# A table that shifts the ranks of 77 groups of instructions before one more ordering pass

## The chip, the cores and the metric

The program runs on one core of a Trainium2 chip. The metric is the time of one execution on the device, in microseconds, as the median of several executions.

A core has five instruction queues that matter here. TensorE (PE) multiplies matrices and transposes, VectorE (DVE), ScalarE (ACT) and GpSimd (POOL) do elementwise work, and SyncE (SP) issues the transfers between memory and the core's buffers. Each works through its own list of instructions in the order in which they were issued, and waits at an instruction until what it reads is there and what it overwrites is no longer needed.

## What is computed

One layer of a streaming encoder, for a prompt of 2048 tokens and a sample of 32 tokens, with a model width of 1024 in float32. The reference, cut down:

```python
def layer(x, mem):
    h = rmsnorm(x, g_pre_mix)
    qa, ka, va, qb, kb, vb, log_a, r = mix_inputs(h, w_in, w_alpha2, b_alpha)
    oa = chunk_band_prompt(qa, ka, va, rel_bias)      # 8 heads x 64, chunks of 64, band of 9 chunks
    ob, state = gla_recurrence(qb, kb, vb, log_a, s0) # 4 heads, keys of 64, values of 128
    x = x + rmsnorm(mix_output(oa, ob, r, g_gla_out, w_o), g_post_mix)
    mk, mv = mem_kv(mem, g_mem, w_mk, w_mv)           # 256 memory tokens
    x = x + rmsnorm(mem_attention(rmsnorm(x, g_pre_mem), mk, mv, w_mq, w_mo), g_post_mem)
    x = x + rmsnorm(swiglu(rmsnorm(x, g_pre_ffn), w_gate, w_up, w_down), g_post_ffn)  # hidden 2816
```

The outputs are both token streams, the new keys and values of both attentions, and the recurrent states.

## The kernel before

**Arithmetic.** A float32 product is done as three matmuls on operands that are split into a rounded part and a remainder (`mm3`, line 531; its matmuls are the rows of L536). `split` (line 494) makes the two parts: ACT casts the rounded part (L495), and DVE or POOL subtracts it from the raw tile for the remainder (L496). `split_own` (L500, L501) does the same in place for the operands of the output projection. The large products use seven sub-products in place of eight, as in Strassen's scheme: sums of operand quarters (L590 and L593, the helpers `sub` and `add`) stand ahead of the splits, and the results land in PSUM tiles called X, Y, Z, T, W.

**Stages, in order of time.** First the combined input projection, to about 525 us. Then the band attention and the gated linear attention together with the output projection, to about 1210; the folding of the memory's keys and values runs between them. Then the memory attention with its norms, to about 1660, and the FFN to the end.

**Names that the prediction speaks of.**
- `g7_j` and `ha2_j`: operands of the memory attention's scores, memory side and token side (`scores_pair`, from line 1753). `hm2_0` and `hm2_1` are the raw tiles that `ha2_j` is split from. `msX`, `msY`, `msZ` are score tiles, `mst` and `mpr` the softmax's minimum and its result (L1784, L1789), `mpt` the transposes of the result on PE (L1793).
- `wo3_6_4_s`: weights of the output projection for token block 3 and output tile 6, second half; `wops3_6_0` is the product (L1464), `om` its token operand, `sqa` and `acc1` the square sums of the norm behind it, and `y1` its result, scaled in L1517.
- `u14_6`: scores plus bias with the running minimum (L1176) for the band attention; `s` are the scores (L1192), `ks` the loaded keys.
- `n3_7` and `n4_7`: the two norms behind the memory attention for the last 256 tokens (`output`, from line 1880). `n4_s7` sums squares on DVE (L593), PE adds over the partitions with a matmul by ones (L1899), ACT takes the root, and `my7_j`, the tokens, are scaled on DVE (L1910), first with `g_post_mem`, later with `g_pre_ffn`. Between the two POOL adds the residual.
- `wg0_2_s0`: split weights of the FFN's gate, block 0, group 2; `pg0_2_X` are its products. `wu` and `pu` are the same for the up projection.
- `mkps`: products for the memory's keys.

**What sets the order.** The program is first written out in the order of its loops. `Order.queue` (line 426) then sorts it anew. It reads all instructions as a graph (`_read`), and plays them through in a planner with an estimated cost for each (`_pass`, line 296): whenever an engine is free, the ready instruction with the lowest priority number starts there. Ten turns of a pass forward and a pass backward over the graph alternate; a backward pass gives the priorities of the next forward pass, as distances from the end, in planned nanoseconds. The forward pass with the earliest planned end is kept. Its planned starts give the order in each engine's list, which is then fixed by a dependency from each instruction to the one before it on its engine. So nothing is reordered while the program runs: an instruction that waits holds up all that is behind it on that engine.

Of the kernel before, what the change touches and what calls it, by code (L numbers as in the profile page):

```python
# [47 lines left out]
class Order:  # L48
# [12 lines left out]
    LOAD = 1280.0  # L61
    TABLES = {1: "natural_log_exp_and_others", 2: "silu_and_others"}
    ROOM = (208 * 1024, 16 * 1024)

    def __init__(self, tc):
        self.tc = tc
        self.block = tc.nc.cur_bb
        self.hints = {}
        self.edge = mybir.DependencyInfo(mybir.DependencyClass.NoSync, mybir.DependencyReason.DATA)
# [124 lines left out]
    def _read(self, traced):  # L194
# [17 lines left out]
        for ins in traced:  # L212
            kind = type(ins).__name__
            eng = str(ins.engine).split(".")[-1]
            if ins.name in opened:
                p, space, size, right = opened[ins.name]
                lo = max([q[2] for q in stack.values() if q[0] == space and not q[3]], default=0)
                if right:
                    lo = min([q[1] for q in stack.values() if q[0] == space and q[3]], default=self.ROOM[space == PSUM]) - size
                stack[p] = (space, lo, lo + size, right)  # L220
# [200 lines left out]
    def behind(self, late, early):  # L421

        for x in late:
            self.hints.setdefault(x.ins.name, []).extend(y.ins.name for y in early)

    def queue(self):
        self._read(self.block.bb.instructions)
        n = len(self.ops)
        best = None
        prio = self.prio  # L430
        for turn in range(self.PASSES + 1):
            start, end = self._pass(prio)
            if best is None or max(end) < best[0]:
                best = (max(end), start)
            if turn == self.PASSES:
                break
            back, fin = self._pass([-(s + d) for s, d in zip(start, self.dur)], back=end)
            whole = max(fin)
            prio = [whole - b for b in fin]
        start = best[1]  # L440
        order = sorted(range(n), key=lambda i: (start[i], i))
        act = [i for i in order if self.eng[i] == 1]
        tail, table, since, loads = {}, 1, 0, {}
        for p, i in enumerate(act):
            if self.table.get(i, table) != table:
                table = self.table[i]
                gaps = [start[act[q]] - start[act[q - 1]] - self.dur[act[q - 1]] for q in range(since, p + 1)]
                room = [g >= self.LOAD for g in gaps]
                loads[act[since + (room.index(True) if True in room else gaps.index(max(gaps)))]] = table
            if i in self.table:  # L450
                since = p + 1
        for i in order:
            e = self.eng[i]
            if e == self.GATE:
                continue
            todo = list(self.ops[i])
            if i in loads:
                todo.insert(0, self.tc.nc.scalar.preload_act_table_set(self.TABLES[loads[i]]).ins)
            for ins in todo:
                if e in tail:  # L460
                    self.tc.add_manual_dep(ins, tail[e].name, self.edge, reason="order of issue")
                tail[e] = ins
# [2124 lines left out]
```

## Time and profile before

| what | value |
|---|---|
| median of 3 runs | 2976.96 us (2975.37 to 2981.22) |
| the profiled execution | 2977.21 us |
| its span, first to last instruction | 2975.4 us |
| mean granted clock of TensorE | 0.994 |
| idle time of PE in the span | 52.8 us |
| transfers | 586.23 MB, 197 GB/s over the span |

Times within the kernel are microseconds from the start of the span. A row of the timeline has the start, the time, the engine, the line, the operation with its output and inputs by name (buffer numbers left out), how many instructions it stands for, and in brackets how long the engine was idle before it and what ended that. A row of the waits has the total, the number of waits and the longest.

### The profile page before, as it was taken

The page shows a single profiled execution, that of the slowest core. Times are in us where ns is not written, and L with a number is a line of the kernel's source. Part 1 is how long each engine was busy: PE and PEld are TensorE (multiplying, and loading weights), DVE is VectorE, ACT ScalarE, POOL GpSimd, SP SyncE. Part 2 cuts the span into 40 slices and gives each one's busy share as a digit, 9 for nine tenths or more (in the row PEclk, how much of TensorE's full clock was granted, in tenths as well). Part 3 has the DMA queues.
Part 4 walks back from the last instruction along what each step waited for, and adds up shares of the span by engine and source line. Part 5 has one row for each costly group of instructions (what it writes and reads, how often), then busy time and mean ns, then how long its engine had stood idle before and what let it go on. Part 6 is the DMA issues. An engine that isn't in the chain of part 4 may idle for free. (4 is left out here: it accounts for less than half of the span.)

```text
span 2975.4 us, 56400 instructions
## 1 busy us (share of the span) xinstructions
PE 2922.6 (98%) x21011; PEld 2753.1 (93%) x21011; DVE 2253.8 (76%) x4156; ACT 1578.4 (53%) x3374; POOL 853.8 (29%) x991
## 2 busy tenths in 40 slices
PE   9999999999999998999999999999999999999999
PEld 7899999888879787878999999999999999999999
DVE  6488876576777867885678977889977778987775
ACT  5565655576767766665445444445443335443334
POOL 0210000456766655222133211114221113321113
PEclk9999999999999999999999999999999999999999
DMA  9645674986778768545994643454554445543344
GB/s 319 203 166 181 219 232 152 301 279 184 251 234 254 238 192 284 185 167 179 344 313 140 192 159 125 170 177 155 179 174 136 146 156 168 160 173 132 132 154 176
DMA packets 429644, 586.23 MB, mean 197 GB/s; under 512 B 49013, under 2 KB 318606, under 8 KB 429338
## 3 DMA queue, kind: packets, MB, share of 16 engines
q1 hardware_dynamic: 428966, 581.93, 59.6%
q8 instruction: 165, 2.70, 0.4%
q14 instruction: 109, 0.89, 0.1%
q10 hardware_dynamic: 404, 0.71, 0.1%
HBM read 426.46 MB, written 160.33 MB: 197 GB/s over the span
## 5 line engine op out<-in xcount | busy, mean ns | idle before, releaser
L496 POOL TENSOR_TENSOR u<-g,u 128x692 fp32r<-128x692 f32 (+1 forms) x109 | 197.0, 1813 | 896.5 <-ACT u L495 849.4
L536 PE MATMUL pg_X<-mf,wg_s 128*128 128x346 f32 (+1 forms) x1584 | 276.8, 322 | 1.4 <-DVE g L593 0.9
L536 PE MATMUL pu_X<-mf,wu_s 128*128 128x346 f32 (+1 forms) x1584 | 274.2, 320 | 0.0
L536 PEld LDWEIGHTS pg_X<-mf,wg_s 128*128 128x128 f32 x1584 | 256.4, 189 | 2.6 <-DVE g L593 1.1
L536 PEld LDWEIGHTS pu_X<-mf,wu_s 128*128 128x128 f32 x1584 | 255.0, 188 | 0.1
L536 PE MATMUL pdX<-u,wd 128*128 128x346 f32 (+1 forms) x1440 | 234.0, 322 | 0.0
L536 PEld LDWEIGHTS pdX<-u,wd 128*128 128x128 f32 x1440 | 230.5, 189 | 0.2
L1464 PE MATMUL wops<-om,wo_s 128*128 128x512 f32 (+1 forms) x960 | 214.6, 363 | 12.5 <-DVE wo_s L496 4.1
L495 ACT CAST wg_s<-wg_r 128x512 fp32r<-128x512 f32 x231 | 136.7, 620 | 168.7 <-DVE wg_r L590 76.6
L495 ACT CAST u<-g 128x692 fp32r<-128x692 f32 (+1 forms) x109 | 82.8, 773 | 229.2 <-PE pdX L536 190.5
L536 PE MATMUL mo<-pT,hT 128*128 128x256 f32 x1536 | 192.3, 285 | 0.7 <-POOL pT L501 0.7
L536 PEld LDWEIGHTS mo<-pT,hT 128*128 128x128 f32 x1536 | 186.7, 192 | 6.4 <-issue 3.3
L495 ACT CAST wu_s<-wu_r 128x512 fp32r<-128x512 f32 x231 | 136.4, 621 | 99.6 <-DVE wu_r L590 43.5
L496 DVE TENSOR_TENSOR wu_s<-wu_r,wu_s 128x512 fp32r<-128x512 f32 x231 | 171.6, 768 | 21.5 <-ACT wu_s L495 21.4
L1464 PEld LDWEIGHTS wops<-om,wo_s 128*128 128x128 f32 x960 | 153.4, 190 | 36.4 <-POOL om L501 5.1
L496 DVE TENSOR_TENSOR wg_s<-wg_r,wg_s 128x512 fp32r<-128x512 f32 x231 | 157.8, 706 | 34.9 <-ACT wg_s L495 34.2
L593 DVE TENSOR_TENSOR acc<-acc,pdX 128x346 f32<-128x346 f32 (+1 forms) x192 | 97.2, 513 | 60.1 <-PE pdX L536 59.6
L536 PE MATMUL pg_Y<-mf,wg_s 128*128 128x346 f32 (+1 forms) x792 | 138.8, 323 | 0.0
L536 PE MATMUL pu_Y<-mf,wu_s 128*128 128x346 f32 (+1 forms) x792 | 136.9, 321 | 0.0
L536 PEld LDWEIGHTS pg_Y<-mf,wg_s 128*128 128x128 f32 x792 | 128.1, 189 | 0.7 <-ACT g L2184 0.3
L536 PEld LDWEIGHTS pu_Y<-mf,wu_s 128*128 128x128 f32 x792 | 127.6, 188 | 0.0
L1379 POOL TENSOR_TENSOR g_W<-g_W,g_kq 128x128 f32<-128x128 f32 x224 | 110.2, 527 | 59.8 <-ACT g_W L1371 49.5
(578 smaller groups left out, 7203.9 us busy)
## 6 DMA issues: line engine op xcount, KB each, us to landing
wd<-wdd SPq DMA_DIRECT2D x182, 512.0 KB, 5.3
wg_r<-in_w_ffn_gate_dram SPq DMA_DIRECT2D x66, 512.0 KB, 4.2
wu_r<-in_w_ffn_up_dram SPq DMA_DIRECT2D x66, 512.0 KB, 4.6
q<-qd SPq DMA_DIRECT2D x32, 512.0 KB, 6.0
wo_r<-in_w_o_dram SPq DMA_DIRECT2D x64, 256.0 KB, 4.2
wdd<-wds SPq DMA_DIRECT2D x28, 512.0 KB, 5.9
wdd<-wd SPq DMA_DIRECT2D x28, 512.0 KB, 4.1
nb<-nbd SPq DMA_DIRECT2D x16, 640.0 KB, 6.6
```

What stands on the lines that cost most here:

```text
L495: ACT.copy(hi, src)
L496: (lo_eng or DVE).tensor_tensor(out=lo, in0=src, in1=hi.bitcast(F32), op=ALU.subtract)
L536: r = PE.matmul(ps, lhsT=a, rhs=b, start=first and i == 0, stop=last and i == len(seq) - 1, skip_group_check=skip)
L593: eng.tensor_tensor(out=out, in0=a, in1=b, op=ALU.add)
L1379: POOL.tensor_tensor(out=wl, in0=wl, in1=both, op=ALU.mult)
L1464: PE.matmul(ps, lhsT=a, rhs=b, start=i == 0, stop=i == len(seq) - 1)
```

## The change

A table gives numbers to 77 groups of instructions, where a group is what one engine writes into one tile (28 on PE, 11 on ACT, 33 on DVE, 2 on POOL, 3 on SP). `_rank` looks an instruction up by its engine and the tile that it writes. The ten turns run as before; then one more forward pass runs with the priorities of the best pass, each plus its number from the table, negative numbers meaning earlier. Its order is issued unless its planned end is later than that of the best pass. The instructions, the tiles and the planned costs are the same. Lines of the code below the table move by 36.

```diff
+    RANKS = {
+        "PE": {
+            "g11_tt": -4400, "gps011": -2150, "hps200": -1400, "hps300": -31200, "mkps0": -37250, "msX1": -350, "msX7": -70800,
...
+        "DVE": {
...
+            "u14_6_sb": -2750, "u14_7_sb": -34600, "u15_6_sb": -13650, "wg0_1_r0": -32200, "wg0_1_s0": -1550, "wg0_1_s1": -32200,
...
+    }
+    def _rank(self, i):
+
+        for a in self.ops[i][0].outs if self.ops[i][0] is not None else ():
+            if hasattr(a, "bass_ap"):
+                return self.RANKS.get(self.ENGINES[self.eng[i]], {}).get(a.bass_ap.tensor.name.rpartition("_")[0], 0.0)
+        return 0.0
+
     def queue(self):
...
             if best is None or max(end) < best[0]:
-                best = (max(end), start)
+                best = (max(end), start, prio)
...
-        start = best[1]
+        start, end = self._pass([p + self._rank(i) for i, p in enumerate(best[2])])
+        if max(end) > best[0]:
+            start = best[1]
```

The pass moves more than the 77 groups, since each place that changes moves the neighbours too: some 3500 of PE's 18985 instructions, 1300 of DVE's 4158, 900 of ACT's 3108, 230 of POOL's and 500 of SP's stand elsewhere than before, most by one or two places. From the FFN's second group of weights on (about 1720 us) the order is the same. Three places follow.

**The scores of the memory attention (1260–1283 us).** DVE before: ha2_0, the first token operand of score pair 2, stands behind the sums of the norm (y1_3, acc1_3) and the softmax of pair 1.

```order
L1787 RECIPROCAL mst1_11_16926<-mst1_11_16926 128x2
L1789 TENSOR_SCALAR mpr1_11_16927<-mpr1_11_16927,mst1_11_16926 128x256 x2
L1787 RECIPROCAL mst1_00_16947<-mst1_00_16947 128x2
L1789 TENSOR_SCALAR mpr1_00_16948<-mpr1_00_16948,mst1_00_16947 128x256 x2
L593 TENSOR_TENSOR acc1_3_15868<-acc1_3_15868,sqb_3_5_16911 128x544
L1787 RECIPROCAL mst1_10_16998<-mst1_10_16998 128x2
L1789 TENSOR_SCALAR mpr1_10_16999<-mpr1_10_16999,mst1_10_16998 128x256
L496 TENSOR_TENSOR ha2_0_17017<-hm2_0_17013,ha2_0_17017 128x512
L590 TENSOR_TENSOR hm2_0_17013<-hm2_0_17013 128x4x128
L593 TENSOR_TENSOR hm2_0_17013<-hm2_0_17013,hm2_1_17014 128x4x128
```

DVE after, from the end of the first minimum search of pair 1 on (the ISA rows, of L1820):

```order
L1820 ISA mst1_01_16875 128x1
L532 TENSOR_TENSOR ha2_0_17017<-hm2_0_17013,ha2_0_17017 128x512
L626 TENSOR_TENSOR hm2_0_17013<-hm2_0_17013 128x4x128
L629 TENSOR_TENSOR hm2_0_17013<-hm2_0_17013,hm2_1_17014 128x4x128
L1820 ISA mpr1_11_16927,mst1_11_16926<-msX1_16802,msc1_1_16806 128x256
L1820 ISA mst1_11_16926 128x1
L1820 ISA mpr1_11_16927,mst1_11_16926<-msX1_16802,msc1_1_16806 128x256
L1820 ISA mst1_11_16926 128x1
L1823 RECIPROCAL mst1_01_16875<-mst1_01_16875 128x2
L1825 TENSOR_SCALAR mpr1_01_16876<-mpr1_01_16876,mst1_01_16875 128x256
L629 TENSOR_TENSOR y1_3_2_15866<-y1_3_2_15866,x0r3_5_16906 128x544
L629 TENSOR_TENSOR acc1_3_15868<-acc1_3_15868,sqb_3_3_16847 128x544
```

The split of ha2_0 and the two sums on hm2_0 have moved ahead of the second minimum search and of what followed it.

PE before, at the same place (msX1, msZ1: scores of pair 1; msX2: those of pair 2):

```order
L536 MATMUL msZ1_16804<-g7_5_16555,ha1_5_16796 128x512 x12
L1793 MATMUL mpt0_10_16891<-ident_61,mpr0_10_16752 128x128 x4
L536 MATMUL msX1_16802<-g7_6_16568,ha1_6_16799 128x512 x12
L1793 MATMUL mpt1_01_16972<-ident_61,mpr1_01_16876 128x128 x2
L536 MATMUL msX2_17042<-g7_0_15735,ha2_0_17017 128x512 x2
L1793 MATMUL mpt1_01_16972<-ident_61,mpr1_01_16876 128x128 x2
L1793 MATMUL mpt1_11_16979<-ident_61,mpr1_11_16927 128x128 x4
L1793 MATMUL mpt1_00_17112<-ident_61,mpr1_00_16948 128x128 x4
L1793 MATMUL mpt1_10_17119<-ident_61,mpr1_10_16999 128x128 x2
L536 MATMUL msX2_17042<-g7_0_15735,ha2_0_17017 128x512 x8
```

PE after:

```order
L572 MATMUL msZ1_16804<-g7_5_16555,ha1_5_16796 128x512 x11
L1829 MATMUL mpt0_10_16891<-ident_61,mpr0_10_16752 128x128 x4
L572 MATMUL msX2_17042<-g7_0_15735,ha2_0_17017 128x512 x6
L572 MATMUL msX1_16802<-g7_6_16568,ha1_6_16799 128x512 x12
L1829 MATMUL mpt1_01_16972<-ident_61,mpr1_01_16876 128x128 x2
L572 MATMUL msX2_17042<-g7_0_15735,ha2_0_17017 128x512 x6
L572 MATMUL msY2_17043<-g7_1_15736,ha2_1_17022 128x512 x5
L1829 MATMUL mpt1_01_16972<-ident_61,mpr1_01_16876 128x128 x2
L572 MATMUL msY2_17043<-g7_1_15736,ha2_1_17022 128x512 x7
L572 MATMUL msX2_17042<-g7_2_15737,ha2_2_17026 128x512 x3
L1829 MATMUL mpt1_11_16979<-ident_61,mpr1_11_16927 128x128 x2
```

The matmuls on ha2_0 and ha2_1 now stand between the transposes of pair 1, where before one group of transposes followed the other.

**The output projection's weights (1205–1210 us).** DVE before, around wo3_6_4_s:

```order
L496 TENSOR_TENSOR g7_4_15739<-gs01_2_15787,g7_4_15739 128x512
L496 TENSOR_TENSOR g7_2_15737<-gs00_2_15786,g7_2_15737 128x512
L590 TENSOR_TENSOR gs10_2_15789<-gs10_2_15789,gs00_2_15786 128x512
L496 TENSOR_TENSOR g7_0_15735<-gs00_3_15809,g7_0_15735 128x512
L593 TENSOR_TENSOR acc1_3_15868<-acc1_3_15868,sqa_3_3_16188 128x544
L496 TENSOR_TENSOR wo3_6_0_s_16387<-wo3_6_0_r_16385,wo3_6_0_s_16387 128x512
L496 TENSOR_TENSOR wo3_6_4_s_16392<-wo3_6_4_r_16390,wo3_6_4_s_16392 128x512
L590 TENSOR_TENSOR gs00_3_15809<-gs01_3_15810,gs00_3_15809 128x512
```

DVE after:

```order
L626 TENSOR_TENSOR gs10_2_15789<-gs10_2_15789,gs00_2_15786 128x512
L532 TENSOR_TENSOR g7_2_15737<-gs00_2_15786,g7_2_15737 128x512
L532 TENSOR_TENSOR g7_4_15739<-gs01_2_15787,g7_4_15739 128x512
L532 TENSOR_TENSOR wo3_6_4_s_16392<-wo3_6_4_r_16390,wo3_6_4_s_16392 128x512
L532 TENSOR_TENSOR wo3_6_0_s_16387<-wo3_6_0_r_16385,wo3_6_0_s_16387 128x512
L629 TENSOR_TENSOR acc1_3_15868<-acc1_3_15868,sqa_3_3_16188 128x544
L532 TENSOR_TENSOR g7_0_15735<-gs00_3_15809,g7_0_15735 128x512
L626 TENSOR_TENSOR gs00_3_15809<-gs01_3_15810,gs00_3_15809 128x512
```

The split of wo3_6_4 has moved ahead of that of wo3_6_0, of the sum into acc1_3 and of g7_0.

**The entry of the FFN (1661–1677 us).** DVE before, from the half sum of n3_s7 to the scalings of my6 and my7:

```order
L593 TENSOR_TENSOR n3_s7_20613<-n3_s7_20613 128x256
L496 TENSOR_TENSOR wg0_2_s0_21487<-wg0_2_r0_21483,wg0_2_s0_21487 128x512
L593 TENSOR_TENSOR n4_s6_20736<-n4_s6_20736,n4_q6_3_20762 128x512
L590 TENSOR_TENSOR wg0_2_r0_21483<-wg0_2_r0_21483 128x4x128
L593 TENSOR_TENSOR wg0_2_r0_21483<-wg0_2_r0_21483,wg0_2_r1_21485 128x4x128
L593 TENSOR_TENSOR n4_s6_20736<-n4_s6_20736 128x256
L1910 SCALAR_TENSOR_TENSOR my7_0_20512<-my7_0_20512,g_post_mem_867,n3_7_20782 128x256
L496 TENSOR_TENSOR wg0_2_s1_21492<-wg0_2_r0_21483,wg0_2_s1_21492 128x512
L590 TENSOR_TENSOR wg0_2_r0_21483<-wg0_2_r1_21485,wg0_2_r0_21483 128x4x128
L1910 SCALAR_TENSOR_TENSOR my7_0_20512<-my7_0_20512,g_post_mem_867,n3_7_20782 128x256
L1910 SCALAR_TENSOR_TENSOR my6_0_20226<-my6_0_20226,g_pre_ffn_869,n4_6_20765 128x256 x4
L1910 SCALAR_TENSOR_TENSOR my7_0_20512<-my7_0_20512,g_post_mem_867,n3_7_20782 128x256 x2
```

DVE after, from the my7 scalings to the split of wg0_2_s1 (the half sum of n3_s7 stands six rows higher):

```order
L1946 SCALAR_TENSOR_TENSOR my7_0_20512<-my7_0_20512,g_post_mem_867,n3_7_20782 128x256 x4
L1946 SCALAR_TENSOR_TENSOR my7_1_20513<-my7_1_20513,g_post_mem_867,n3_7_20782 128x256 x2
L629 TENSOR_TENSOR g0_1_21217<-pg0_1_c0_21253,pg0_1_Z_21252 128x348
L1946 SCALAR_TENSOR_TENSOR my7_1_20513<-my7_1_20513,g_post_mem_867,n3_7_20782 128x256 x2
L1946 SCALAR_TENSOR_TENSOR my6_0_20226<-my6_0_20226,g_pre_ffn_869,n4_6_20765 128x256 x4
L1946 SCALAR_TENSOR_TENSOR my6_1_20227<-my6_1_20227,g_pre_ffn_869,n4_6_20765 128x256 x4
L532 TENSOR_TENSOR wg0_2_s0_21487<-wg0_2_r0_21483,wg0_2_s0_21487 128x512
L626 TENSOR_TENSOR wg0_2_r0_21483<-wg0_2_r0_21483 128x4x128
L629 TENSOR_TENSOR wg0_2_r0_21483<-wg0_2_r0_21483,wg0_2_r1_21485 128x4x128
L629 TENSOR_TENSOR n4_s7_20793<-n4_s7_20793,n4_q7_1_20801 128x512
L629 TENSOR_TENSOR n4_s7_20793<-n4_s7_20793,n4_q7_2_20810 128x512
L532 TENSOR_TENSOR wg0_2_s1_21492<-wg0_2_r0_21483,wg0_2_s1_21492 128x512
```

The eight scalings of my7 stand together, and the splits and sums of wg0_2 have moved behind them and behind the my6 scalings.

PE before, from the matmuls ahead of n3_7 to n4_7:

```order
L536 MATMUL pg0_1_Z_21252<-mf0_5_20948,wg0_1_s5_21244 128x348 x12
L536 MATMUL pg0_1_X_21250<-mf0_6_20952,wg0_1_s6_21247 128x348 x12
L536 MATMUL pu0_1_X_21379<-mf0_2_20939,wu0_1_s2_21363 128x348 x9
L1899 MATMUL n3_7_20782<-n3_s7_20613,ones_63 128x256
L536 MATMUL pu0_1_X_21379<-mf0_2_20939,wu0_1_s2_21363 128x348
L536 MATMUL pu0_1_Y_21380<-mf0_3_20942,wu0_1_s3_21367 128x348 x12
L536 MATMUL pu0_1_X_21379<-mf0_4_20945,wu0_1_s4_21370 128x348 x5
L1899 MATMUL n4_6_20765<-n4_s6_20736,ones_63 128x256
L536 MATMUL pu0_1_X_21379<-mf0_4_20945,wu0_1_s4_21370 128x348 x7
L536 MATMUL pg0_2_X_21512<-mf0_0_20930,wg0_2_s0_21487 128x348 x12
L536 MATMUL pg0_2_X_21512<-mf0_2_20939,wg0_2_s2_21496 128x348 x2
L1899 MATMUL n4_7_20822<-n4_s7_20793,ones_63 128x256
```

PE after:

```order
L572 MATMUL pg0_1_X_21250<-mf0_6_20952,wg0_1_s6_21247 128x348 x12
L1935 MATMUL n3_7_20782<-n3_s7_20613,ones_63 128x256
L572 MATMUL pu0_1_Y_21380<-mf0_1_20934,wu0_1_s1_21359 128x348 x2
L572 MATMUL pg0_1_Z_21252<-mf0_5_20948,wg0_1_s5_21244 128x348 x12
L1935 MATMUL n4_6_20765<-n4_s6_20736,ones_63 128x256
L572 MATMUL pu0_1_X_21379<-mf0_2_20939,wu0_1_s2_21363 128x348 x12
L572 MATMUL pu0_1_Y_21380<-mf0_3_20942,wu0_1_s3_21367 128x348 x12
L572 MATMUL pu0_1_X_21379<-mf0_4_20945,wu0_1_s4_21370 128x348 x12
L572 MATMUL pg0_2_X_21512<-mf0_0_20930,wg0_2_s0_21487 128x348 x12
L572 MATMUL pg0_2_X_21512<-mf0_2_20939,wg0_2_s2_21496 128x348 x2
L1935 MATMUL n4_7_20822<-n4_s7_20793,ones_63 128x256
```

n3_7 has moved ahead of pg0_1_Z and pu0_1_X; n4_7 still stands behind the first two matmuls of wg0_2_s2.

More of the change, by code (lines that the diff above doesn't have):

```diff
@@ L63 @@
     ROOM = (208 * 1024, 16 * 1024)
+    RANKS = {
[6 rows of a table added]
+        },
+        "Activation": {
+            "om1_4": -56200, "om1_5": -4600, "om3_7": 2050, "po12_3_rec": 850, "po9_0_rec": -14550, "prt15_0": -10500,
+            "prt15_1": -138350, "prt8_0": -3850, "wo2_7_4_s": -10850, "wva0_s10": -10400, "wva1_c1": -42100,
+        },
+        "DVE": {
[6 rows of a table added]
+        },
+        "Pool": {
+            "acc1_2": -41600, "om1_5": -3550,
+        },
+        "SP": {
+            "q0_0": -950, "wva0_r00": -5050, "x0_01": -9750,
+        },
+    }
     def __init__(self, tc):
```

9 rows, old and new, of the table RANKS are left out of this document.

## The prediction

> **What bounds the kernel now.** I read the page first: the share of each engine, then the chain that ended last.
>
> ```profile
> span 2975.4 us, 56400 instructions
> ...
> PE 2922.6 (98%) x21011; PEld 2753.1 (93%) x21011; DVE 2253.8 (76%) x4156; ACT 1578.4 (53%) x3374; POOL 853.8 (29%) x991
> ...
> PE 43%; DVE 0%; DMA 0%; ACT 0%; POOL 0%; POOLq 0%; issue 0%; SPq 0%; ACTq 0%
> ```
>
> TensorE (PE) is busy for 2922.6 of 2975.4 us, so it is idle for 52.8 us. Both programs hold the same matmuls, so a new order can win only from these 52.8 us and from matmuls that run stretched behind a gap. The windows say where they lie. Their columns are length, busy time of PE, of its weight loads, of DVE, ACT and POOL, then the granted clock, the DMA share and GB/s.
>
> ```profile
> 525.00:560.00 35.00, 30.66 (x330) 27.03 (x329) 15.16 (x46) 18.02 (x53) 13.16 (x35) 0.95 0.96 301
> 600.00:1000.00 400.00, 392.19 (x4191) 334.74 (x4189) 292.12 (x782) 282.56 (x786) 262.89 (x458) 1.00 0.77 242
> 1100.00:1300.00 200.00, 182.03 (x1086) 152.16 (x1085) 160.31 (x299) 124.70 (x285) 75.07 (x50) 0.96 0.67 218
> 1650.00:1725.00 75.00, 68.83 (x415) 67.69 (x414) 64.29 (x117) 32.91 (x62) 20.90 (x14) 0.95 0.69 233
> 2300.00:2925.00 625.00, 625.00 (x3938) 624.18 (x3937) 487.27 (x786) 256.97 (x469) 130.84 (x84) 1.00 0.47 157
> ```
>
> The FFN (the last row) has no gap, and its order does not change. The idle time sits in 1100–1300 (18.0 us), 600–1000 (7.8), 1650–1725 (6.2) and 525–560 (4.3). PE's waits say for whom (total, times, longest):
>
> ```profile
> PE n L1899 <- DVE n_s L593: 5.6, 1, 5.6
> PE wops L1464 <- DVE wo_s L496: 4.1, 2, 2.9
> PE wops L1464 <- POOL om L501: 3.8, 3, 2.4
> ```
>
> These are single stalls behind one operation of VectorE (DVE) or GpSimd (POOL) that came late in its engine's fixed order. So I price each by what now stands ahead of that operation.
>
> **The change, place by place.** No instruction comes or goes, so every term is a wait.
>
> (a) **Scores of the memory attention, 1269–1283.**
>
> ```profile
> 1269.44 0.63 PE L1793 MATMUL mpt<-ident,mpr 128*128 128x128 f32 x4 [1.06 <-DVE mpr L1789]
> 1271.00 0.66 PE L1793 MATMUL mpt<-ident,mpr 128*128 128x128 f32 x4 [0.93 <-ACT mps L1796]
> 1272.38 0.69 PE L1793 MATMUL mpt<-ident,mpr 128*128 128x128 f32 x2 [0.72 <-DVE ha L496]
> 1272.72 3.41 PE L536 MATMUL msX<-g,ha 128*128 128x512 f32 x8
> ...
> 1276.65 2.96 PE L536 MATMUL msY<-g,ha 128*128 128x512 f32 x12
> ...
> 1282.85 0.62 PE L1494 MATMUL sqb_ps<-acc,ones 128*128 128x272 f32 x2
> 1271.68 0.68 DVE L496 TENSOR_TENSOR ha<-hm,ha 128x512 fp32r<-128x512 f32 x1
> ```
>
> Transposes of softmax columns stood one behind another (1.06 + 0.93 + 0.72 = 2.71 us idle). The matmuls that could fill the gaps waited for the split of ha2_0, which DVE reached only at 1271.68. In the new order that split comes ahead of the minimum searches on msX1 and of the y1_3 and acc1_3 sums. PE now has 27 of the ha2 matmuls ahead of the first mpt1_11 (6, 6, 5, 7 and 3 in the rows), where it had 2. At 2.96 / 12 = 0.25 us each that is 6 us more cover, for 2.71. I take all of it, and the stretch behind the gaps: eight msX matmuls took 3.41 us where eight at 0.25 take 2.0, so 1.4. The sums that move back are read only at 1282.85, by the square sum's matmul, behind more PE work than they move; if that cover is gone, the wait comes back there, and the gain is 0. **−4.1 us** (bounds −4.1 and 0).
>
> (b) **Output projection, 1206–1213.**
>
> ```profile
> 1209.62 4.04 PE L1464 MATMUL wops<-om,wo_s 128*128 128x272 f32 x20 [2.88 <-DVE wo_s L496]
> ...
> 1206.51 0.72 DVE L593 TENSOR_TENSOR acc<-acc,sqa 128x544 f32<-128x544 f32 x1
> 1207.14 2.42 DVE L496 TENSOR_TENSOR wo_s<-wo_r,wo_s 128x512 fp32r<-128x512 f32 x2
> ...
> 1206.00:1213.00 7.00, 4.12 (x23) 3.90 (x24) 7.00 (x8) 2.30 (x4) 3.40 (x2) 0.84 0.37 131
> 1266.00:1277.00 11.00, 8.29 (x37) 6.31 (x36) 9.18 (x19) 5.21 (x15) 3.15 (x2) 0.84 0.59 198
> 1677.00:1681.00 4.00, 4.00 (x13) 3.55 (x14) 3.23 (x7) 2.88 (x6) 0.00 (x0) 0.50 0.25 57
> ```
>
> The remainder of wo3_6_4 was the second of the two (2.42 us together), behind an acc sum of 0.72. Now it comes ahead of wo3_6_0, acc1_3 and g7_0, so about 2 us earlier. Its cast on ACT still waits its turn, so I take 1.7 of the 2.88. The granted clock was 0.84: 0.16 × 4.12 = 0.7 us lost, of which 1.7 / 2.88 comes back, 0.4. **−2.1** (−3.6 to 0).
>
> Behind gaps of at most 1.06 and 2.88 us the granted clock of these rows is 0.84, and behind the gap of 5.64 us it is 0.50. The Trainium skill, "TensorE: Matmul & The Clock Gate", section "What's actually happening", says that the array falls to half rate after an idle window of some 3.4 us and recovers after as long a busy one. By that rule only the gap of 5.64 us would stretch the matmuls behind it, and the sum would lack the 1.4 and the 0.4, so be 1.8 us smaller; the trace's 0.84 behind shorter gaps speaks against so sharp a threshold.
>
> (c) **The entry of the FFN, 1661–1690**, the longest stall.
>
> ```profile
> 1676.80 1.22 PE L1899 MATMUL n<-n_s,ones 128*128 128x256 f32 x2 [5.64 <-DVE n_s L593]
> ...
> 1673.94 1.35 DVE L593 TENSOR_TENSOR n_s<-n_s,n_q 128x512 f32<-128x512 f32 x1
> 1675.61 0.68 DVE L593 TENSOR_TENSOR n_s<-n_s,n_q 128x512 f32<-128x512 f32 x1
> ...
> 1667.48 1.30 POOL L593 TENSOR_TENSOR my<-my,x1r 128x512 f32<-128x512 f32 x1 [6.61 <-DVE my L1910]
> 1670.57 4.17 POOL L593 TENSOR_TENSOR my<-my,x1r 128x512 f32<-128x512 f32 x3 [1.80 <-ACT pg_c L676]
> ...
> 1668.79 3.78 DVE my L1910 x10
> ...
> 1655.00:1677.00 22.00, 15.82 (x97) 15.15 (x96) 20.15 (x39) 10.68 (x21) 7.26 (x6) 0.95 0.61 192
> ```
>
> The row of 3.78 us is from the chain of waits: ten `my` scalings back to back on DVE, then the n4_s7 sums, then PE. The change puts n3_7, which the my7 scalings read, ahead of 24 matmuls that stood before it (12 of pg0_1_Z and 12 of pu0_1_X), at 0.17 us about 4 us. It also puts the eight my7 scalings together and the operations on wg0_2 behind them. That shortens a chain that is bound by latency. But DVE was idle for only 22.00 − 20.15 = 1.9 us from 1655 to 1677, and one more 128x512 operation (wu0_1_s5, 0.7) now stands ahead of n4_s7, so that n4_s7 can end only 1.2 us earlier. Behind it, five my7 scalings that followed the split of wg0_2_s5 now precede it: 5 × 0.38 (3.78 / 10), less the 0.7 that was done earlier, is 1.2 us later for pg0_2_Z. **0** (−5.64 and half of the 4 us at clock 0.50, so −7.6, if the whole stall goes; the upper end, +9, is worked out as a rival).
>
> (d) **Band attention, 1121–1129.**
>
> ```profile
> 1121.89 1.27 PE L1192 MATMUL s<-ks,q 128*128 128x320 f32 x4 [0.92 <-DVE u_mn L1176]
> 1125.62 0.83 PE L1192 MATMUL s<-ks,q 128*128 128x320 f32 x4
> 1128.32 0.41 PE L1192 MATMUL s<-ks,q 128*128 128x320 f32 x1 [1.54 <-DVE u_mn L1176]
> ```
>
> The softmax reads u14_6 and u15_6 now precede the long scalings of y1_2. The scores that u15_6 reads ended at 1126.45, and PE waited for it until 1128.32; a little over a microsecond is free there. **−1.2** (−0.92 − 1.54 = −2.5 to 0).
>
> (e) **Start of the band attention, 525–560.**
>
> ```profile
> 544.60 0.63 PE L1192 MATMUL s<-ks,q 128*128 128x128 f32 x4 [1.70 <-DMA ks<-kad]
> 535.53 3.10 PE L1464 MATMUL mkps<-mm,wmk_s 128*128 128x256 f32 x24 [0.52 <-DVE mkf L1540]
> 539.49 1.40 SPq L1341 DMA_DIRECT2D g_kq<-kbd  x1
> ```
>
> All 24 mkps2 matmuls now stand ahead of these scores, where 10 did: 14 × 3.10 / 24 = 1.8 us of work for a stall of 1.70. But SP issues the key load behind the g_kq load that followed it; of the 1.40 us that it took I count 0.5, since part of it was a full queue. −1.3 is left. **−1.3** (−4.3, all idle time of 525–560, to +1.4).
>
> (f) **984–989: 0.**
>
> ```profile
> 988.15 0.72 PE L1464 MATMUL wops<-om,wo_s 128*128 128x512 f32 x2 [2.43 <-POOL om L501]
> 986.64 2.69 POOL L501 TENSOR_TENSOR om<-om 128x512 fp32r<-128x512 f32 x2
> ```
>
> om2_2 moves well ahead on POOL. But om2_3, the second of the two, has as much POOL work ahead of it as before, and its matmuls now stand next on PE: the wait is handed on (−2.4 to 0).
>
> (g) **The rest.** In 600–1000 the 7.8 us of idle time are many small pieces, and as many consumers come closer to their producers as move away; the start is reordered a little. 0, bounds ±3.
>
> Sum: −4.1 − 2.1 + 0 − 1.2 − 1.3 = **−8.7 us**. The profiled execution took 2977.21 us, 1.8 more than its span and 0.25 above the median of 2976.96; that median less 8.7 is 2968.3.
>
> **Rivals.** *The waits only move* (2974 us). Place (f) is the pattern: an engine that is busy without a gap, as DVE was for all of 1206–1213, only trades one delay for the next. Then (b), (d) and (e) give nothing, and (a) gives 2.7: 2974. Against it: in (a) the delayed sums have slack. Chance 0.31.
>
> *The chain, not DVE's queue, sets (c)* (2963 us). Then n4_s7 gains the 4 us of n3_7, half of the slow clock's 2 us goes with it, and the sum is −8.7 − 5 = −13.7. For it: ten `my` scalings are the chain. Against it: the 1.9 us of idle time. With (b), (d) and (e) whole (−5.8 more) it comes to 2957.5, with (f) to 2955. Chance 0.08.
>
> *Collisions with POOL at the entry of the FFN* (slower). A sum of 128x512 took 1.35 us beside POOL's adds and 0.68 after them. In the old order POOL was idle for 6.61 us before 1667.48, just when DVE worked on wg0_2; in the new order five such operations (the splits of wg0_2_s0 and wg0_2_s1 and three sums) run beside POOL's four adds. At +0.67 each that is 3.4 us, at a whole add of POOL each (4.17 / 3 = 1.39) 7.0. With the 0.7 of the extra operation n4_s7 ends up to 7.7 us later, and with the 1.2 behind it (c) costs +9. It makes the kernel slower from where (a), (b), (d) and (e) give less than 3: 2977 + 9 − 3 = 2983. Chance 0.13. The Trainium skill, "SBUF — State Buffer", section "Who interferes with whom", says that a DVE operation with two SBUF inputs and a GpSimd operation that reads SBUF exclude each other, the later one waiting for the whole instruction. The trace agrees in kind (1.35 against 0.68), though 0.67 is half of one add.
>
> That the change does nothing, the extra pass being thrown away, is excluded: the issued order differs.
>
> **How the numbers follow.** 2968.3 us has the remaining chance, 0.48. A measurement of this kernel tells about 0.2% (6 us) from no change. Faster: 0.48 + 0.08 = 0.56. Within 0.2%: the moved waits, 0.31. Slower: 0.13. The range begins at the low end of the chain case, 2955, and ends at 2980, inside the slower case, most of which is left out.
>
> **What would show it.** PE's waits for mpr, mps and ha near 1270 gone; the wait for wo_s near 2.4; that for n_s still over 3.5; a wait for om near 985 as before. The forecast is wrong if n_s falls below 2 us (chain), if it grows while DVE's 128x512 operations there take over 1.3 us (collision), or if the unchanged FFN changes its time.

## The result and the profile after

The changed kernel took 2963.71 us (median of 4 runs, 2959.66 to 2966.28) against 2978.72 for the kernel before beside it (4 runs): a ratio of 0.9949, 95% interval 0.9932 to 0.9966, or some 15 us. Two later timings of the same kernel gave 0.9949 and 0.9946. The forecast of 2968.3 has the sign and more than half of the size.

The page of the changed kernel: span, busy times, the chain that ended last.

```profile
span 2962.1 us, 56382 instructions
...
PE 2918.8 (99%) x21011; PEld 2749.1 (93%) x21011; DVE 2255.0 (76%) x4156; ACT 1576.7 (53%) x3374; POOL 849.8 (29%) x991
...
PE 58%; DVE 1%; DMA 1%; ACT 0%; POOL 0%; issue 0%; SPq 0%; DVEq 0%; ACTq 0%
```

PE is idle for 43.3 us, where it was for 52.8, and busy for 3.8 us less with the same 21011 matmuls. The rest of what came back is clock: matmuls that no longer run stretched behind a gap. The windows of the changed kernel, at the same times as those shown of before (the same columns). They hold a little later work, since the changed kernel is up to 14 us ahead in them:

```profile
525.00:560.00 35.00, 32.60 (x354) 28.33 (x353) 16.32 (x49) 19.27 (x56) 13.10 (x36) 1.00 0.94 299
600.00:1000.00 400.00, 391.34 (x4216) 334.39 (x4215) 295.35 (x786) 283.47 (x788) 261.88 (x458) 1.00 0.77 244
1100.00:1300.00 200.00, 189.12 (x1132) 158.27 (x1131) 167.76 (x309) 128.13 (x286) 77.03 (x51) 0.98 0.69 227
1650.00:1725.00 75.00, 71.70 (x436) 70.20 (x435) 62.68 (x117) 31.91 (x61) 19.29 (x13) 0.98 0.60 209
2300.00:2925.00 625.00, 625.00 (x3945) 624.10 (x3944) 486.29 (x786) 258.91 (x471) 134.36 (x86) 1.00 0.47 157
```

In 1100–1300 PE's idle time falls from 18.0 to 10.9 us and the clock rises from 0.96 to 0.98; in 1650–1725 it falls from 6.2 to 3.3, the clock from 0.95 to 0.98. In 600–1000 nothing is won (7.8 before, 8.7 now), and the FFN is as it was. PE's waits in the changed kernel (total, times, longest):

```profile
PE pg_X L572 <- ACT wg_s L531: 3.0, 1, 3.0
PE wops L1500 <- POOL om L537: 3.0, 4, 1.5
PE pt L1256 <- ACT prt L1258: 2.6, 2, 1.6
...
PE wops L1500 <- DVE wo_s L532: 1.7, 3, 0.7
...
PE g_e L1406 <- DVE g_laR L532: 1.4, 1, 1.4
```

The 5.6 us for n_s are gone; at the same place now stand 3.0 for wg_s. The longest wait for wo_s fell from 2.9 to 0.7. The last row is new. In the timeline, PE at the scores of the memory attention (a) and at the entry of the FFN (c):

```profile
1261.27 0.38 PE L1829 MATMUL mpt<-ident,mpr 128*128 128x128 f32 x2
1261.40 1.66 PE L572 MATMUL msX<-g,ha 128*128 128x512 f32 x6
1262.89 1.33 PE L572 MATMUL msY<-g,ha 128*128 128x512 f32 x5
1264.07 0.38 PE L1829 MATMUL mpt<-ident,mpr 128*128 128x128 f32 x2
...
1662.20 0.59 PE L572 MATMUL pg_X<-mf,wg_s 128*128 128x348 f32 x2 [2.98 <-ACT wg_s L531]
1662.62 0.69 PE L1935 MATMUL n<-n_s,ones 128*128 128x256 f32 x2
```

In (a) the ha2 matmuls stand between the transposes, with no wait in brackets. In (c) n4_7 comes right behind the one wait that is left.

**Where the time came from.** Two profiles of one order differ by several us, so I counted leads over all profiles of this study. For PE's matmuls that start within 8 us behind a border in the profile of before, I took the median of their start in a run less their start before; the lead of a stretch is the difference between its two borders (us, negative is won). "Whole table" is the three profiles of the changed kernel; "old order" is the profile of before (zero by definition) and those of experiments whose order in that stretch is the one of before.

| stretch | term, forecast | whole table | old order, lowest to highest | difference of means |
|---|---|---|---|---|
| 0–500 | (g) | −0.2 to +1.4 | 0 to +1.2 | −0.1 |
| 500–670 | (e) −1.3 | −3.5 to −5.0 | −3.7 to 0 | −1.8 |
| 670–770 | (g) | +1.6 to +1.7 | −0.1 to +0.5 | +1.5 |
| 770–1010 | (f) 0 | −1.2 to −4.1 | −3.1 to 0 | −0.7 |
| 1010–1190 | (d) −1.2 | −2.7 to −3.8 | −0.2 to +2.5 | −3.9 |
| 1190–1225 | (b) −2.1 | −2.3 to −2.5 | −0.1 to +1.1 | −2.9 |
| 1225–1310 | (a) −4.1 | −5.2 to −5.4 | 0 | −5.3 |
| 1310–1450 | (g) | +1.4 to +2.0 | 0 to +1.6 | +1.5 |
| 1600–1710 | (c) 0 | −3.0 to −3.4 | −0.4 to +0.2 | −3.1 |
| the rest | (g) | | | −0.7 |

The last column adds up to −15.5 us; the three timings gave some −15 to −16. Where the old order's leads spread over several us (500–670, 770–1010), a difference of means below 2 is not told apart from the difference between executions.

### The profile page after: what moved, and what is told of

Its sections match the earlier page's. It is cut to its first block, busy times and chain, and to the rows that moved or that the text cites. A ratio compares the mean times of both kernels' runs of the same rounds, so it can differ in the third digit from the quotient of the medians.

```text
span 2962.1 us, 56382 instructions
## 1 busy us (share of the span) xinstructions
PE 2918.8 (99%) x21011; PEld 2749.1 (93%) x21011; DVE 2255.0 (76%) x4156; ACT 1576.7 (53%) x3374; POOL 849.8 (29%) x991
## 4 chain that ended last, share of the span: by engine, by line
PE 58%; DVE 1%; DMA 1%; ACT 0%; POOL 0%; issue 0%; SPq 0%; DVEq 0%; ACTq 0%
PE pu_X L572 8%; PE pg_X L572 8%; PE pdX L572 8%; PE mo L572 6%; PE pg_Y L572 4%; PE pu_Y L572 4%; PE pdY L572 4%; PE msX L572 3%; PE pu_Z L572 2%; PE pdZ L572 2%; PE pg_Z L572 2%; PE msY L572 2%; PE pdn L572 1%; PE wops L1500 1%; PE msZ L572 1%; DMA gs<-gd 0%
```

## The experiments

Each is the changed kernel with another table. The last pass is thrown away by line 475 of the changed kernel, `if max(end) > best[0]`, where the planner's own estimate calls it longer; in e2, e4, e8, e9 and e10 that line and the next are taken out, so that the small tables take effect. Ratios are to the kernel before in the same series, with 95% intervals.

**e1, the entry of the FFN alone.** Only the thirteen groups of (c); the order differs from before only from 1600 us on.

```diff
-        "PE": { ...28 groups... }, "Activation": {...}, "DVE": { ...33 groups... }, "Pool": {...}, "SP": {...}
+        "PE": {"n3_7": -17850, "pg0_1_X": -51400, "pg0_2_Y": -114550, "pu0_2_X": -17850, "pu0_2_Y": -14450},
+        "DVE": {"my6_0": -2550, "my6_1": -549800, "my7_0": -138100, "my7_1": -12650, "wg0_1_r0": -32200,
+                "wg0_1_s0": -1550, "wg0_1_s1": -32200, "wg0_2_s0": 5000},
```

> Only the 13 groups of the entry of the FFN keep their numbers (my6, my7, wg0_1, wg0_2, n3_7, pg0_1_X, pg0_2_Y, pu0_2_X, pu0_2_Y); up to 1600 us the order is that of before. Theory 1 (DVE's queue is the bound there, and the new order wins because its 128x512 operations no longer run beside POOL's adds): PE arrives 3.1 us sooner behind 1690 us, as in the changed kernel, DVE's operations between 1655 and 1677 have at most one over 0.9 us, and the time is 3 us shorter (2975 against 2978). Theory 2 (the gain at the entry came from what was moved upstream): 0 to 1 us.

**e2, the same without the number of wg0_2_s0**, which holds wg0_2's splits and sums behind the my6 scalings. Without it they come beside POOL's adds.

```diff
-                "wg0_1_s0": -1550, "wg0_1_s1": -32200, "wg0_2_s0": 5000},
+                "wg0_1_s0": -1550, "wg0_1_s1": -32200},
...
-        if max(end) > best[0]:
-            start = best[1]
```

> As e1 but without the number of wg0_2_s0: the same my7 scalings and norm matmuls, but the splits and sums on wg0_2 stand right behind the my7 scalings, beside POOL's adds, instead of behind the my6 scalings. Theory 1 (collisions with POOL): two to four of these operations take 1.0 to 1.7 us instead of 0.69, n4_s7 ends 2 to 4 us later than in e1 (0.7 of it for one more operation ahead of it), and most of the 3 us is lost. Theory 2 (the order on DVE's queue alone): only the 0.7 us is lost, all operations at 0.69.

Measured: e1 2973.31 us, 0.9988 [0.9979, 0.9998]; e2 2979.11, 1.0008 [0.9998, 1.0018]. In 1600–1710 e1 has a lead of −3.3, e2 of +1.8. The timeline of DVE and POOL in e1, then in e2, and the windows from the half sum of n3_s7 to the end of n4_s7:

```profile
1666.82 3.22 DVE L1928 SCALAR_TENSOR_TENSOR my<-my,g_pre_ffn,n 128x256 f32<-128x256 f32 x8
...
1670.67 0.69 DVE L608 TENSOR_TENSOR wg_r<-wg_r 128x512 f32<-128x512 f32 x1
1671.40 0.69 DVE L611 TENSOR_TENSOR wg_r<-wg_r,wg_r 128x512 f32<-128x512 f32 x1
...
1664.26 3.81 POOL L611 TENSOR_TENSOR my<-my,x1r 128x512 f32<-128x512 f32 x3 [14.38 <-DVE my L1928]
1668.69 1.30 POOL L611 TENSOR_TENSOR my<-my,x1r 128x512 f32<-128x512 f32 x1 [0.63 <-DMA x1r<-x1d]
...
1660.18:1675.87 15.69, 12.47 (x76) 11.74 (x74) 15.45 (x34) 8.84 (x18) 5.21 (x5) 1.00 0.61 185
```

```profile
1663.72 1.67 DVE L606 TENSOR_TENSOR wg_r<-wg_r 128x512 f32<-128x512 f32 x1
1665.42 1.67 DVE L609 TENSOR_TENSOR wg_r<-wg_r,wg_r 128x512 f32<-128x512 f32 x1
...
1660.44 4.40 POOL L609 TENSOR_TENSOR my<-my,x1r 128x512 f32<-128x512 f32 x3 [14.38 <-DVE my L1926]
1665.01 1.53 POOL L609 TENSOR_TENSOR my<-my,x1r 128x512 f32<-128x512 f32 x1 [0.17 <-DMA x1r<-x1d]
...
1656.36:1674.41 18.05, 13.45 (x79) 12.76 (x78) 17.91 (x35) 9.04 (x18) 6.03 (x5) 0.96 0.51 161
```

The two sums on wg_r take 0.69 us behind POOL's adds and 1.67 beside them. DVE needs 2.46 us more for one more operation (0.68 of it); n4_s7 ends 2.4 us later in the stretch. So the collisions are real, and the changed kernel is on the good side of them. They are not the whole 5.1 us between the two leads: the rest arises at PE, which is idle for 7.0 us in e2's stretch and for 3.2 in e1's, with a wait of 2.39 us for g behind n4_7, and which runs at half the clock for 6.8 us in place of 3.4. That these follow from the later n4_s7 was not tried.

**e3, the five numbers of ha2 and hm2 alone**, for (a).

```diff
+        "DVE": {"ha2_0": -11550, "ha2_1": -11400, "ha2_2": -24400, "ha2_3": -8750, "hm2_0": -37500},
```

> Only the five numbers of ha2 and hm2 on DVE are kept. Theory 1 (the early split of ha2_0 gives PE matmuls to put between the transposes): the waits for mpr, mps and ha near 1270 are gone and PE is 4 to 5.4 us ahead from 1300 us on; time 4 to 5 us shorter. Theory 2 (the waits only move, to the sums behind): at most 2 us.

Measured: 2974.26 us, 0.9987 [0.9977, 0.9996]; lead in 1225–1310 −3.3, where the whole table has −5.4. The windows of before, e3 and the changed kernel, one row of each:

```profile
1255.00:1290.00 35.00, 31.94 (x142) 25.14 (x141) 30.55 (x58) 19.77 (x48) 14.33 (x10) 0.95 0.56 186
```

```profile
1255.00:1290.00 35.00, 33.99 (x158) 26.66 (x157) 31.52 (x68) 21.99 (x55) 11.09 (x8) 1.00 0.49 171
```

```profile
1255.00:1290.00 35.00, 35.00 (x171) 28.61 (x170) 30.89 (x72) 24.23 (x60) 10.32 (x7) 1.00 0.51 183
```

The five numbers alone bring back the clock and two thirds of the 3.06 us of idle time, less than the 4 to 5.4 us of lead that were expected. The other 1.01 us need the other numbers of the stage (msX1, msZ0, y1_3_2 and acc1_3 start there); which of them was not tried.

**e4, wo3_6_4 alone**, for (b), and **e9, all ten numbers of 1160–1220**.

```diff
+        "DVE": {"wo3_6_4_s": -96150},                                                                    # e4
+        "PE": {"hps200": -1400, "hps300": -31200, "wops3_3_1": -135950},                                 # e9
+        "DVE": {"acc1_3": 950, "g7_0": 1800, "g7_4": 3450, "gs00_2": 1400, "wo3_6_4_s": -96150,
+                "wo3_7_0_s": 10000, "y1_3_2": -25000},
...
-        if max(end) > best[0]:
-            start = best[1]
```

> Only the number of wo3_6_4_s on DVE is kept. Theory 1 (its place in DVE's queue): PE is 2.1 to 2.4 us ahead behind 1215 us, its wait for wo_s falls from 2.88 to under 1 us. Theory 2 (another operation of the same queue becomes the next wait): under 1 us ahead.

> Only the ten numbers of the groups that start between 1160 and 1220 us (wo3_6_4_s as in e4, and wo3_7_0_s, hps200, hps300, acc1_3, g7_0, g7_4, gs00_2, y1_3_2, wops3_3_1). In e4 the number of wo3_6_4_s alone left a new wait of 2.02 us for the copy of y1_3 and PE 0.5 us ahead. Theory 1 (the other numbers clear DVE's queue for that copy): 2.2 to 2.5 us ahead from 1190 to 1225, as in the whole table, no wait over 1 us there. Theory 2 (the lead needs what was moved before 1160): under 1.5 us.

Measured: e4 2976.73 us, 0.9998 [0.9986, 1.001]; e9 2975.27, 0.9994 [0.9985, 1.0003]. Leads in 1190–1225: e4 −0.45, a little below the old order's lowest (−0.1); e9 −2.5, all that the whole table has. Some of e9's ten numbers change the order in 1225–1310 too, and there it gives 1.0 back. PE in the timeline of e4, then of e9:

```profile
1214.82 3.46 PE L1476 MATMUL wops<-om,wo_s 128*128 128x272 f32 x13 [2.02 <-DVE y L1518]
```

```profile
1204.97 6.67 PE L1480 MATMUL wops<-om,wo_s 128*128 128x272 f32 x48 [0.77 <-ACT wo_s L511]
...
1216.02 6.01 PE L1480 MATMUL wops<-om,wo_s 128*128 128x272 f32 x46 [0.69 <-DVE wo_s L512]
```

Alone, the earlier split only trades the wait for wo_s for one of 2.02 us for y; the nine other numbers are what leaves pieces under 0.8. The times of both cannot be told from before: 2.5 us is 0.08% of the kernel.

**e8, u14_6, u14_7 and u15_6 alone**, for (d), and **e10, all eight numbers of 1010–1160**.

```diff
+        "DVE": {"u14_6_sb": -2750, "u14_7_sb": -34600, "u15_6_sb": -13650},                              # e8 and e10
+        "PE": {"ss_7": -4850},                                                                           # e10
+        "Activation": {"om3_7": 2050, "po12_3_rec": 850, "wo2_7_4_s": -10850},
+        "Pool": {"acc1_2": -41600},
...
-        if max(end) > best[0]:
-            start = best[1]
```

> Only the numbers of u14_6, u14_7 and u15_6 on DVE are kept. Theory 1 (as predicted: the softmax reads ahead of the y1_2 scalings): the two waits for u_mn of 0.92 and 1.54 us fall, PE 1 to 2 us ahead behind 1190 us. Theory 2 (DVE is full there, and the scalings moved back make hst or wo_s late): the waits for hst and wo_s between 1140 and 1160 grow by as much, 0 us.

> Only the eight numbers of the groups between 1010 and 1160 us (u14_6, u14_7, u15_6 as in e8, and acc1_2 on POOL, wo2_7_4_s, po12_3_rec and om3_7 on ACT, ss_7 on PE). e8 left PE 1.05 us ahead from 1110 to 1190, the whole table 3 to 4. Theory 1 (POOL's and ACT's numbers bring the rest: acc1_2 and wo2_7_4_s): 2.5 to 4 us ahead there, the wait for hst of 2.2 us down to about 1.3. Theory 2 (the rest comes from other places or is a difference between executions): about 1 us.

Measured: e8 2974.21 us, 0.9995 [0.9986, 1.0004]; e10 2973.82, 0.9991 [0.9982, 1.0]. Leads in 1110–1190: e8 −1.1, e10 −2.3, whole table −3.0 to −4.0, old order −0.1 to +1.4. The next wait behind the band attention, in the timeline of before, of e8 and of e10:

```profile
1143.35 2.93 PE L536 MATMUL hps<-wov_s,vt 128*128 128x512 f32 x6 [2.04 <-DVE hst L1599]
```

```profile
1138.59 2.93 PE L548 MATMUL hps<-wov_s,vt 128*128 128x512 f32 x6 [2.60 <-DVE hst L1611]
```

```profile
1137.45 2.93 PE L557 MATMUL hps<-wov_s,vt 128*128 128x512 f32 x6 [1.29 <-DVE hst L1620]
```

The three softmax reads win about what (d) said, but not free of charge: PE's waits for u_mn of 0.92 and 1.54 us shrink to one of 0.71 (and one of 0.54 for o), while that for hst grows from 2.04 to 2.60 and that for sprt from 0.63 to 1.19. The other five numbers of e10 add 1.2 us, about what the wait for hst has lost (2.60 to 1.29 and one more of 0.30). The whole table has 0.7 to 1.7 us beyond e10. Part of it is PE's wait of 1.08 us for wo_s at 1178 in e10, where the changed kernel waits 0.47 and 0.17 for y; the rest was not traced. The time of e8 cannot be told from before, and that of e10 hardly.

**e5 and e12, the changed kernel again, e7, all but the entry, and e6 and e11, without numbers that seemed to lose.**

```diff
 # e7: without n3_7, pg0_1_X, pg0_2_Y, pu0_2_X, pu0_2_Y, my6_0, my6_1, my7_0, my7_1, wg0_1_r0, wg0_1_s0, wg0_1_s1, wg0_2_s0
 # e6: without the six
-            "msX7": -70800,   "s7_2_1": -4550,   "wva0_s10": -10400,   "x0_10": 1000,   "wva0_r00": -5050,   "x0_01": -9750,
 # e11: without the first two only
-            "msX7": -70800,   "s7_2_1": -4550,
```

> The changed kernel once more, beside e6. The profiles of e1 to e4 show that places with one and the same order differ between executions: from 500 to 575 us they were 2.2 to 3.5 us ahead of the profile of before, unchanged. If the changed kernel's lead of 2.8 us there is only such a difference, its lead at the other places should come back here within 1 us (1110 to 1190: 2.5; 1190 to 1225: 2.3; 1225 to 1310: 5.4; 1620 to 1710: 3.1), and the time is 0.4 to 0.6% shorter. If those were differences between executions too, they come out elsewhere and the time is within 0.3% of before.

> The table without the 13 groups of the FFN's entry, the complement of e1. If the places add up: 3 to 4 us slower than e5, so about 11 us faster than before, with the 5.64 us wait for n_s back. If e1's gain depends on the rest: more or less than that by over 2 us.

> The whole table without the numbers behind three places where the changed kernel fell back: the start (x0_01, wva0_r00, x0_10, wva0_s10), s7_2_1 and msX7. Theory 1 (those places lose what the profile showed: 0.8 at the start, 1.4 at 675 to 720, 1.4 near 1400): 2 to 3.5 us faster than e5. Theory 2 (these were differences between executions): within 1 us of e5.

> The whole table without s7_2_1 and msX7. In e6 the place at 670 to 770 was 1.3 us ahead where the table left it 1.64 behind in three executions, and 1350 to 1450 level where the table left it 1.4 to 4.2 behind. Theory 1 (these are two losing numbers): 3 to 5 us faster than e12, so about 0.65% faster than before. Theory 2 (what they save comes back as a wait later on): within 1 us of e12.

> The changed kernel a third time, beside e11, for the comparison: 0.5% faster than before; 670 to 770 us 1.6 us behind, 1350 to 1450 us 1 to 2 us behind, 1225 to 1310 5.2 to 5.4 us ahead.

Measured, e5, e7 and e6 in one series: 2960.55 us, 0.9949 [0.9937, 0.9962]; 2968.40, 0.9968 [0.9956, 0.998]; 2960.89, 0.9946 [0.9934, 0.9959]. e11 and e12 in another: 2956.93, 0.9931 [0.9919, 0.9943]; 2962.52, 0.9946 [0.9933, 0.9958].

In e5 the leads of the first profile came back within 0.3 us in 1190–1225, 1225–1310 and 1600–1710; in 1110–1190 it was 4.0, 1.0 more.

e7 shows (c) from the other side: its lead in 1600–1710 is −0.4. It times 7.9 us above e5, over 2 us more than the 3 to 4 expected, which was to mean that e1's gain depends on the rest. The profiles do not bear that out: the entry itself makes 3.0. Of the rest, 2.4 lie in 1310–1450 and 1.6 in 1110–1190, where both have the same order (they part at 1620 us), and I take them for a difference between executions. Above the other two timings of the changed kernel, e7 lies 4.7 and 5.9 us.

The whole table loses 1.5 us in each of two stretches, 670–770 and 1310–1450. PE at both in e12, then in e11:

```profile
681.46 0.73 PE L1406 MATMUL g_e<-tall,g_laR 128*128 128x512 f32 x2 [1.39 <-DVE g_laR L532]
...
1400.44 1.82 PE L572 MATMUL mo<-pT,hT 128*128 128x256 f32 x13 [2.36 <-POOL pT L537]
```

```profile
676.99 0.63 PE L1406 MATMUL g_e<-tall,g_laR 128*128 128x512 f32 x2
...
1393.89 8.29 PE L572 MATMUL mo<-pT,hT 128*128 128x256 f32 x67 [0.71 <-POOL pT L537]
```

Without s7_2_1 the wait for g_laR is gone and 670–770 turns from +1.7 to −1.2; without msX7 the one for pT shrinks and 1310–1450 goes from +2.0 to +0.2. The second case is the weaker one. The wait for pT is 0.71 or 0.72 us in the profiles without msX7 and 0.92 to 2.36 in the four with it, but in the first profile of the changed kernel it is 0.92 only and a wait of 1.24 for a transfer (s_hq) stands beside it; and e1, with the old order, lost 1.6 us there too, behind a wait of 1.37 for mps. Together 4.7 us in the profiles, 5.6 between the medians: **e11 is the fastest version of this study**, though its interval overlaps that of e12. e6 contains the same two edits and timed no better than e5. Its profile has the gain at both places too, and gives it back in 0–670 (+0.8, against −4.6 in e5 and −4.1 in e11). Whether the four start numbers that it lacks are worth that, or the one profile was a late one, stays open.

## Why the prediction was right, and what it missed

(a) **Right, a little small.** The waits for mpr, mps and ha are gone and the clock is back. Idle time of 3.06 us in 1255–1290 came back where 2.71 was counted, and 0.05 × 31.94 = 1.6 us of clock where 1.4 was; that is 4.7 of the 5.3. The other 0.6 are not accounted for. e3 shows that the five numbers on ha2 and hm2 carry two thirds; that the split of ha2_0 alone does was not tried.

(b) **Right in size, wrong in what does it.** The wait for wo_s fell as said, and 1190–1225 won 2.9 for 2.1. But the text gave it to one split; e4 shows that alone it does what the rival "the waits only move" says. The price was that of a row, the cause a group of ten. The price of the clock was too small: the slow stretch runs on to 1214.12, past the end of the window that the 0.7 was read from, and half of its 3.40 us is 1.7 at most. In the changed kernel the clock is 1.00 in all of 1190–1225.

(c) **The step that failed**, and the largest part of the missing time. It kept every duration and asked only how much idle time DVE had: "n4_s7 can end only 1.2 us earlier", given back behind it, so 0. DVE was indeed the bound (its idle time only went from 1.99 to 1.16 us), but its busy time was not fixed. The windows of before and of the changed kernel over the same work, from the same instruction to the end of n4_s7:

```profile
1640.00:1676.74 36.74, 30.62 (x190) 29.94 (x188) 34.75 (x62) 17.76 (x35) 11.89 (x9) 0.98 0.54 167
```

```profile
1628.65:1662.55 33.90, 30.68 (x190) 29.95 (x188) 32.74 (x63) 17.07 (x34) 11.47 (x9) 1.00 0.64 195
```

63 operations take 2.0 us less than 62 did. Which ones, the groups of these windows say, shape by shape (count, busy time, mean ns of one), before and then now:

```profile
L496 DVE TENSOR_TENSOR wg_s<-wg_r,wg_s 128x512 fp32r<-128x512 f32 x9 | 7.0, 784 | 0.4 <-ACT wg_s L495 0.4
L1910 DVE SCALAR_TENSOR_TENSOR my<-my,g_post_mem,n 128x256 f32<-128x256 f32 x15 | 6.7, 472 | 0.0
L593 DVE TENSOR_TENSOR n_s<-n_s,n_q 128x512 f32<-128x512 f32 x7 | 5.7, 810 | 0.0
L496 DVE TENSOR_TENSOR wu_s<-wu_r,wu_s 128x512 fp32r<-128x512 f32 x5 | 4.4, 883 | 0.3 <-ACT wu_s L495 0.3
```

```profile
L1946 DVE SCALAR_TENSOR_TENSOR my<-my,g_post_mem,n 128x256 f32<-128x256 f32 x15 | 6.2, 475 | 0.0
L532 DVE TENSOR_TENSOR wg_s<-wg_r,wg_s 128x512 fp32r<-128x512 f32 x9 | 6.1, 685 | 0.0
L629 DVE TENSOR_TENSOR n_s<-n_s,n_q 128x512 f32<-128x512 f32 x7 | 5.1, 722 | 0.1
L532 DVE TENSOR_TENSOR wu_s<-wu_r,wu_s 128x512 fp32r<-128x512 f32 x6 | 4.0, 686 | 0.7 <-ACT wu_s L531 0.7
```

9 × 0.099 + 5 × 0.197 + 7 × 0.088 = 2.5 us less on splits and sums, both of whose inputs lie in SBUF. The scalings, one of whose inputs is the matmul result n in PSUM, kept their time (472 and 475 ns). The Trainium skill, "SBUF — State Buffer", section "Who interferes with whom", says that a DVE operation with at most one SBUF input, outside its two-port modes, does not contend with GpSimd; the trace agrees. In the old order three splits lay under POOL's adds on my6, between 1644 and 1661 (1.60, 1.39 and 0.97 us in place of 0.69), two of them ahead of 1655, where the prediction began to count, and two sums of n4_s7 under those on my7 (0.91 and 1.35). In the changed kernel all four adds on my7 run beside scalings, which keep their time. The collision rival named this mechanism, but it misread the order: the five operations on wg0_2 that it puts under the adds stand behind the my6 scalings, and all ran at 0.69 us from 1656.62 on, when POOL's last add ended (1656.44). And it did not look at the operations that would leave the adds. e1 against e2 shows the mechanism with either sign. The test "n_s below 2 us means the chain" would have misled: the wait for n_s is gone by name, since two matmuls in front of it wait 2.98 us for wg_s, and n4_s7 still ends when DVE is done. The measured time, 2963.7, is that of the chain rival (2963), but not by its sum: DVE stayed the bound in (c), and 2.7 us more came from (d) and 2.0 from (a) and (b). That the two times meet is chance.

(d) **About right for its three reads** (e8: −1.1, and −1.2 said, in one profile, where the old order alone spreads over 1.5); the stage won 3.9, since numbers that the text did not price shorten the waits behind them too. e10 shows that for the wait for hst; a part stays untraced.

(e) **Not told apart.** The wait for ks is gone from the top of the list, and the profiles are 3.5 to 5.0 ahead there; but those with the old order are 2.1 to 3.7 ahead too, since the one profile that the prediction was read from is the last of them all there. The difference, −1.8, is near the −1.3. No row shows that part of the 1.40 us of the g_kq load was a full queue; what bears out the 0.5 is that the g_kq load ahead of the key load takes 0.43 in the changed kernel.

(f) **Half wrong.** A wait for om near 985 was to stay at 2.43; it is 0.58 (and in e12 gone), and another of 1.59 for prt (0.42 in e5, 1.78 in e12) stands 11 us ahead of it. In PE at this place, now:

```profile
977.20 0.66 PE L1256 MATMUL pt<-ident,u_sb 128*128 128x128 f32 x4 [1.59 <-ACT prt L1258]
...
988.32 0.73 PE L1500 MATMUL wops<-om,wo_s 128*128 128x512 f32 x2 [0.58 <-POOL om L537]
```

The stretch as a whole (−0.7) cannot be told from the 0.

(g) **Within its ±3**, though not by being nothing: +1.5 twice, the two losses that e11 takes out.

One reading of the clock that (b) builds on needs a correction: the 0.84 of its rows is the mean over a window, no level. Cut at the places where it changes, the granted clock in these profiles is 1.00 or 0.50 (rows in the last section). The gap of 2.88 us was followed by 3.40 us at 0.50, and so were the three of 1.06, 0.93 and 0.72 together, so it was right to count stretched matmuls there.

So −8.7 became −15.5 in the leads: 3.1 more from (c), 2.7 from (d) and its unpriced neighbours, 2.0 from (a) and (b), 1.2 from (e) and (f), which may be chance, less 2.2 for (g).

## What to carry to other kernels

When a reorder is priced, ask not only what now stands ahead of a late operation but also what runs beside it on the other engines: on an engine that is busy throughout, which operations overlap decides how long its work is. One moved instruction need not win alone (e4): the wait was passed on until those behind it were moved as well (e9). And a single profile is no baseline for terms of 1 to 3 us: profile the old order a few times first and use the places where the executions agree.

## What the runs showed of the hardware that was not expected

- A sum of 128x512 on DVE with both inputs in SBUF takes 0.69 us alone and up to 1.67 beside POOL's adds; POOL's three adds went from 3.81 to 4.40 us in the same place. The scalings with one input in PSUM kept 0.47 to 0.48.
- With the same order, eight executions differ by up to 3.7 us in 500–670 and 3.1 in 770–1010, and seven by some 0.6 in 1600–1710.
- The granted clock is 1.00 or 0.50; means between, such as 0.84, come of windows that cut across a change. Behind the gap of 2.98 us at 1662 it stays at 1.00 for 1.7 us, is 0.50 for 3.41 us and 1.00 again; before, it was 0.50 for 3.40 us behind the gap of 2.88 that ends at 1209.62, and for 6.82 us from within the gap of 5.64 on. So behind a shorter gap the slow stretch was half as long, but it was there.
- It can also fall where PE has no gap at all. In e1 it is 0.50 for 3.40 us behind 32 matmuls of 128x32 that took 3.65 us; before, with the same matmuls at the same place, it stayed at 1.00. e11 has the same stretch, and each of the two loses 1.6 us by it in 1450–1600.

A row of the changed kernel, of before and of e1 (the clock is the number behind POOL's busy time):

```profile
1663.92:1667.33 3.41, 3.33 (x12) 2.88 (x11) 3.24 (x8) 3.38 (x7) 0.00 (x0) 0.50 0.43 106
```

```profile
1210.72:1214.12 3.40, 3.40 (x16) 3.31 (x15) 3.37 (x6) 1.83 (x3) 0.00 (x0) 0.50 0.25 95
```

```profile
1489.13:1492.53 3.40, 3.40 (x15) 3.23 (x15) 1.60 (x5) 2.82 (x6) 0.65 (x1) 0.50 1.06 331
```
